# Both parts of x as one 512-column moving operand in the up projection of a decoder layer, with the residual's scale and offset in quarters

## The chip, the cores and the metric

The program runs on one core of a Trainium2 chip. The metric is the device time of one execution in microseconds (us), as a median of several runs. The engines in this text: PE does the matmuls (PEld its weight loads), DVE is the vector engine, ACT the scalar engine, POOL the GpSimd, and SP issues most of the DMAs. Each engine works through its own queue in order and waits on semaphores for the others.

## The reference, cut to what matters

One layer with sequence 256 and width 1024; everything is float32.

```python
x = layer_norm(ALPHA * x + mix, ln1_g, ln1_b)            # mix: attention, conv and pooling heads times w_out
up = causal_dwconv(x @ w_up, ffn_conv_w) + ffn_conv_b    # 1024 -> 2 * 2816, then width-3 taps along the sequence
u, g = split(up, 2)
ff = (u * silu(g)) @ w_down                              # 2816 -> 1024
x = layer_norm(ALPHA * x + ff, ln2_g, ln2_b)
```

## The kernel before

**Precision.** A product of float32 matrices is made from parts. `split(raw, hi, lo)` (lines 121 to 123) writes `hi`, a copy rounded to the fast matmul format, on ACT and `lo = raw - hi` on DVE. `mm3` (line 149) then issues three matmuls: hi by hi, hi by lo, lo by hi. So each weight tile of 128x1024 costs one ACT instruction (line 122) and one DVE instruction (line 123), and x itself is held as `xh` and `xl`.

**The up projection.** It has 22 column blocks j, each with two halves: s = 0 for u and s = 1 for g. `up_mm(j, s)` (line 460) runs over k = 0..7 with the weight part as the stationary 128x128 operand and 256 columns of `xh` or `xl` moving: 3 x 8 matmuls into one half of a PSUM bank, and u and g of one j share that bank. Block 0 is made apart (`up_first`), in plain float32, right after the first LayerNorm.

**The taps and the gate.** `taps(j, s)` (line 480) reads the bank: ACT writes `y` from it (line 485), DVE adds the two delayed taps, again from the bank (lines 486, 487). `gate_silu` (ACT, line 491) and `gate_out` follow: DVE makes `f` (line 495), ACT rounds it into `mh` (line 122), DVE makes `ml` (line 123).

**The down projection.** `down(k, t, p)` uses `mh[k]` and `ml[k]` as stationary operand and 512 columns of the down weights as moving operand. It trails the up projection by five blocks. For the last seven blocks only rows t = 0 are done at once. The matmuls of rows t = 1 for these blocks come in three pieces at the very end, and block 21 is the last in each.

**What sets the order.** The program is written as a list of blocks, each with its PE work, then work for the other engines that is written behind the PE work of the next block (`late`, lines 653 to 667): first the taps of the block before, then as many weight splits (`wsplit`) as a look-ahead of seven blocks asks for, then the gate. So on ACT and on DVE the taps, the weight splits and the gate of one j stand in a fixed order. From j = 6 to j = 20 three weight tiles are split for each j, from j = 1 to 5 and for j = 21 two.

**The first LayerNorm.** `ln1_rows` (DVE) normalises, `ln1_turn` (PE) transposes into PSUM, `ln1_cols` applies scale and offset by column into `xf` (line 444 on ACT for rows t = 0, line 446 on DVE for rows t = 1), `ln1_split` writes `xh` and `xl`. Beside that, `ln1_x` (lines 453, 454) applies scale and offset to the residual rows `xr` on POOL, one multiply and one add of 128x1024 for each t. `xr` is next read at the end, in the second LayerNorm's residual (line 360).

Of the kernel before, what the change touches and what calls it, by code (L numbers as in the profile page):

```python
# [17 lines left out]
P = 128  # L18
# [38 lines left out]
def trunk(ctx, tc, a_qk, a_v, a_cp, a_out, a_up, a_down, x, par, tab, lnp, out):  # L57
# [8 lines left out]
    def bank():  # L66
        return ps.tile([P, 512], F32, name="bank")
# [86 lines left out]
    tb = cp.tile([NB + 1, GW + NH], F32, name="tb")  # L154
    xh = cp.tile([P, KD, S], F32R, name="xh")
    xl = cp.tile([P, KD, S], F32R, name="xl")

# [263 lines left out]

    def ln1_rows(t):
        mv = norm_stats(t)
        for c in range(0, D, S):
            nc.vector.tensor_scalar(xr[:, t, c:c + S], xr[:, t, c:c + S], mv[:, 0:1], mv[:, 2:],
                                    op0=ALU.subtract, op1=ALU.mult)
# [9 lines left out]
    def ln1_cols(t, hf):  # L436

        ts = slice(t * P, (t + 1) * P)
        for i in range(4):
            k = 4 * hf + i  # L440
            src = t_ps[t, hf][:, i * P:(i + 1) * P]
            g, b = (prm[:, C_LN + r * KD + k:C_LN + r * KD + k + 1] for r in range(2))
            if t == 0:
                nc.scalar.activation(xf[:, k, ts], src, AF.Identity, scale=g, bias=b)
            else:
                nc.vector.tensor_scalar(xf[:, k, ts], src, g, b, op0=ALU.mult, op1=ALU.add)
# [4 lines left out]

    def ln1_x(t):
        nc.gpsimd.tensor_mul(xr[:, t], xr[:, t], gb[0][:, 0])  # L453
        nc.gpsimd.tensor_add(xr[:, t], xr[:, t], gb[0][:, 1])

# [3 lines left out]

    def up_mm(j, s):  # L460
        h, l = W.pop(("ug"[s], j))
        if s == 0:
            u_ps[j] = bank()
        for k in range(KD):
            ws = slice(k * P, (k + 1) * P)
            mm3(u_ps[j][:, s * S:(s + 1) * S], h[:, ws], l[:, ws], xh[:, k], xl[:, k], k == 0, k == KD - 1)

# [12 lines left out]
    def taps(j, s):  # L480
        c = s * NJ + j
        w = [prm[:, C_FW + 3 * c + i:C_FW + 3 * c + i + 1] for i in range(3)]
        src = u_ps[j][:, s * S:(s + 1) * S]
        y = ys[j, s] = tmp(f"y{s}")
        nc.scalar.activation(y, src, AF.Identity, scale=w[2], bias=prm[:, C_FB + c:C_FB + c + 1])  # L485
        nc.vector.scalar_tensor_tensor(y[:, 1:], src[:, :S - 1], w[1], y[:, 1:], op0=ALU.mult, op1=ALU.add)  # L486
        nc.vector.scalar_tensor_tensor(y[:, 2:], src[:, :S - 2], w[0], y[:, 2:], op0=ALU.mult, op1=ALU.add)  # L487
# [104 lines left out]
    for i in range(FIRST):  # L592
# [4 lines left out]
    block(L(w_out_last, 1, 0), (), [L(rs, 1, 0)])  # L597
    block(seq(L(ln1_turn, 0, 0), L(w_out_last, 1, 1)), (), [L(ln1_cols, 0, 0), L(rs, 1, 1)])
    block(seq(L(ln1_turn, 0, 1), L(w_out_last, 1, 2)), (),
          [L(ln1_cols, 0, 1), L(rs, 1, 2), L(ln1_rows, 1)], now=True, more=False)  # L600
    steps = list(enumerate((k, s) for s in range(2) for k in range(KD)))
    block(seq(L(up_first, 0, steps[:12]), L(ln1_turn, 1, 0)), (),
          [L(ln1_cols, 1, 0)], now=True, more=False)
    block(seq(L(up_first, 0, steps[12:]), L(ln1_turn, 1, 1)), (),
          [L(ln1_cols, 1, 1)] + [L(ln1_split, t, hf) for hf in range(2) for t in range(NT)],
          now=True, more=False)
# [134 lines left out]
```

## Time and profile before

| what | value |
| --- | --- |
| device time, 3 runs | median 294.5 us (293.94, 294.5, 296.25) |
| the profiled execution | 293.62 us, of which the span of the trace is 291.8 us |
| PE busy | 282.5 us, 97% of the span |
| PEld busy | 260.8 us, 89% |
| DVE busy | 222.7 us, 76% |
| ACT busy | 157.8 us, 54% |
| POOL busy | 41.1 us, 14% |
| TensorE clock granted | 0.996 of full speed |
| HBM read | 54.89 MB at a mean of 192 GB/s |

Matmuls overlap, so a matmul's own duration (282 ns for 256 columns) is longer than the step from one start to the next, and it is the step that counts. The busy share is over the whole span: what DVE and ACT do within the up projection has to be read from a stretch of it.

### The profile page before, as it was taken

The page shows a single profiled execution, that of the slowest core. Times are in us where ns is not written, and L with a number is a line of the kernel's source. Part 1 is how long each engine was busy: PE and PEld are TensorE (multiplying, and loading weights), DVE is VectorE, ACT ScalarE, POOL GpSimd, SP SyncE. Part 2 cuts the span into 40 slices and gives each one's busy share as a digit, 9 for nine tenths or more (in the row PEclk, how much of TensorE's full clock was granted, in tenths as well). Part 3 has the DMA queues.
Part 4 walks back from the last instruction along what each step waited for, and adds up shares of the span by engine and source line. Part 5 has one row for each costly group of instructions (what it writes and reads, how often), then busy time and mean ns, then how long its engine had stood idle before and what let it go on. Part 6 is the DMA issues. An engine that isn't in the chain of part 4 may idle for free.

```text
span 291.8 us, 5033 instructions
## 1 busy us (share of the span) xinstructions
PE 282.5 (97%) x2034; PEld 260.8 (89%) x2034; DVE 222.7 (76%) x384; ACT 157.8 (54%) x261; POOL 41.1 (14%) x43
## 2 busy tenths in 40 slices
PE   8999999999999999999999999999999999999990
PEld 7899779988888999999999999999999999999880
DVE  2876575797947699998988888888767867768575
ACT  3864746856512294266766666666555665665100
POOL 1020004860000279900000000000000000000011
PEclk9999999999999999999999999999999999999998
DMA  7999951234990169273737474847374552100011
GB/s 258 405 358 418 418 213 46 101 146 153 337 350 25 46 207 387 84 290 144 287 146 275 159 287 144 290 146 290 144 286 147 186 227 86 77 2 0 0 75 72
DMA packets 9367, 56.28 MB, mean 193 GB/s; under 512 B 1069, under 2 KB 1333, under 8 KB 3712
## 3 DMA queue, kind: packets, MB, share of 16 engines
q1 hardware_dynamic: 7920, 50.99, 46.5%
q0 software_dynamic: 1136, 4.58, 4.4%
q10 hardware_dynamic: 288, 0.39, 0.4%
q8 instruction: 16, 0.26, 0.3%
q14 instruction: 7, 0.06, 0.1%
HBM read 54.89 MB, written 1.06 MB: 192 GB/s over the span
## 4 chain that ended last, share of the span: by engine, by line
PE 79%; DVE 8%; ACT 4%; issue 4%; DMA 2%; POOL 1%; POOLq 0%; SPq 0%; DVEq 0%
PE bank L151 75%; DVE lo L123 3%; PE bank L474 2%; DMA raw<-a_qk 2%; DVE pr L242 2%; ACT pr L234 2%; ACT hi L122 2%; DVE lg L231 1%; PE bank L434 1%; PE bank L261 1%; DVE stat L366 1%; DVE xr L360 0%; DVE xr L521 0%; POOLq L737 0%; POOL mv L399 0%
## 5 line engine op out<-in xcount | busy, mean ns | idle before, releaser
L123 DVE TENSOR_TENSOR lo<-raw,hi 128x1024 fp32r<-128x1024 f32 (+2 forms) x95 | 113.8, 1210 | 23.6 <-ACT hi L122 23.3
L151 PE MATMUL bank<-xh,hi 128*128 128x256 f32 x462 | 130.3, 282 | 0.2 <-ACT hi L122 0.2
L151 PE MATMUL bank<-xh,lo 128*128 128x256 f32 x462 | 129.1, 279 | 0.2 <-DVE lo L123 0.2
L151 PE MATMUL bank<-xl,hi 128*128 128x256 f32 x462 | 129.0, 279 | 0.0
L122 ACT ACTIVATE hi<-raw 128x1024 fp32r<-128x1024 f32 (+2 forms) x95 | 95.4, 1018 | 4.5 <-DMA raw<-a_v 2.2
L151 PEld LDWEIGHTS bank<-xh,hi 128*128 128x128 f32 x462 | 87.1, 188 | 2.3 <-ACT hi L122 1.2
L151 PEld LDWEIGHTS bank<-xl,hi 128*128 128x128 f32 x462 | 87.1, 188 | 0.7
L151 PEld LDWEIGHTS bank<-xh,lo 128*128 128x128 f32 x462 | 87.0, 188 | 0.4 <-DVE lo L123 0.4
L151 PE MATMUL bank<-hi,mh 128*128 128x512 f32 (+1 forms) x133 | 49.3, 371 | 0.0
L151 PE MATMUL bank<-lo,mh 128*128 128x512 f32 (+1 forms) x133 | 49.2, 370 | 0.0
L151 PE MATMUL bank<-hi,ml 128*128 128x512 f32 (+1 forms) x133 | 49.0, 368 | 0.0
L485 ACT ACTIVATE y<-bank,prm 128x256 f32<-128x256 f32 x44 | 24.6, 559 | 25.8 <-PE bank L151 13.6
L399 POOL TENSOR_TENSOR mv<-mv,half 128x1 f32<-128x1 f32 x4 | 3.1, 774 | 186.3 <-DVE mv L398 186.3
L151 PEld LDWEIGHTS bank<-hi,ml 128*128 128x128 f32 x133 | 25.1, 188 | 4.3
L151 PEld LDWEIGHTS bank<-hi,mh 128*128 128x128 f32 x133 | 25.1, 189 | 3.7
L151 PEld LDWEIGHTS bank<-lo,mh 128*128 128x128 f32 x133 | 25.1, 188 | 3.5
L486 DVE SCALAR_TENSOR_TENSOR y<-bank,prm,y 128x255 f32<-128x255 f32 x44 | 21.0, 478 | 8.7 <-ACT y L485 8.6
L487 DVE SCALAR_TENSOR_TENSOR y<-bank,prm,y 128x254 f32<-128x254 f32 x44 | 21.2, 481 | 1.6
L122 ACT ACTIVATE mh<-f 128x256 fp32r<-128x256 f32 x22 | 9.2, 418 | 24.3 <-DVE f L495 24.3
L123 DVE TENSOR_TENSOR ml<-f,mh 128x256 fp32r<-128x256 f32 x22 | 11.0, 500 | 10.6 <-ACT mh L122 10.6
L491 ACT ACTIVATE sg<-y 128x256 f32<-128x256 f32 x22 | 9.2, 419 | 13.8 <-DVE y L487 13.8
L453 POOL TENSOR_TENSOR xr<-xr,lnp 128x1024 f32<-128x1024 f32 x2 | 13.4, 6702 | 3.1 <-DMA lnp<-lnp 3.1
(93 smaller groups left out, 201.9 us busy)
## 6 DMA issues: line engine op xcount, KB each, us to landing
raw<-a_up SPq DMA_DIRECT2D x22, 1024.0 KB, 4.8
raw<-a_down SPq DMA_DIRECT2D x11, 1024.0 KB, 5.6
raw<-a_qk SPq DMA_DIRECT2D x7, 640.0 KB, 7.2
raw<-a_cp SPq DMA_DIRECT2D x4, 1024.0 KB, 14.5
raw<-a_out SPq DMA_DIRECT2D x4, 1024.0 KB, 5.2
raw<-a_v SPq DMA_DIRECT2D x2, 1024.0 KB, 8.3
lnp<-lnp POOLq DMA_DIRECT2D x4, 512.0 KB, 4.6
bias<-g_dr POOLq DMA_DIRECT2D x1, 1024.0 KB, 13.6
```

Of the source, the lines that this page charges most:

```text
L122: nc.scalar.activation(hi, raw, AF.Copy)
L123: nc.vector.tensor_sub(lo, raw, hi.bitcast(F32))
L151: nc.tensor.matmul(o, l, r, start=start and i == 0, stop=stop and i == 2, skip_group_check=skip)
L234: nc.scalar.activation(pr[:, a:b], lg[:, a:b], AF.Exp, bias=st[:, t:t + 1], scale=-1.0, accum_out=st[:, 2 + t:3 + t])
L242: nc.vector.tensor_scalar(pr[:, a:b], pr[:, a:b], st[:, 4 + t:5 + t], None, op0=ALU.mult)
L399: nc.gpsimd.tensor_tensor(mv[:, 2:], mv[:, 2:], half, op=ALU.pow)
L453: nc.gpsimd.tensor_mul(xr[:, t], xr[:, t], gb[0][:, 0])
L474: nc.tensor.matmul(u_ps[0][:, c:c + P], part(("ug"[s], 0))[:, k * P:(k + 1) * P], xf[:, k, t * P:(t + 1) * P], start=t == 0 and n == 0, st ...
L485: nc.scalar.activation(y, src, AF.Identity, scale=w[2], bias=prm[:, C_FB + c:C_FB + c + 1])
L486: nc.vector.scalar_tensor_tensor(y[:, 1:], src[:, :S - 1], w[1], y[:, 1:], op0=ALU.mult, op1=ALU.add)
L487: nc.vector.scalar_tensor_tensor(y[:, 2:], src[:, :S - 2], w[0], y[:, 2:], op0=ALU.mult, op1=ALU.add)
L491: nc.scalar.activation(ys[j, 2], ys.pop((j, 1)), AF.Silu)
```

## The change

The two parts of x now stand side by side in one tile, `xp[P, k, part, S]`, and `xh` and `xl` are its two views. In `up_mm` the hi part of the weights is loaded once for each k and multiplied by 512 moving columns, hi and lo of x together, into a whole bank. The lo part of the weights is multiplied by 256 columns, the hi part of x, into the first half of that bank. The bank then holds two partial sums side by side. `taps` adds them: ACT copies the second half to `e`, DVE adds `e` to the first half in the bank, and then the three tap instructions follow as before. Each (j, s) has a bank of its own. The residual's scale and offset are written in quarters of 256 columns behind the blocks j = 8 to 15, and the parameters of the second LayerNorm are loaded behind block 16. In the first LayerNorm, `ln1_cols` for rows t = 1 alternates between DVE and ACT, and the two `ln1_split` of rows t = 0 stand earlier.

```diff
--- before.py
+++ after.py
@@ -37,6 +37,7 @@
 KEEP = 7
 FIRST = 2
 WARM = 23
+LATE = 8
 
 
 PIECES = (((0, 512), (512, 512)), ((0, 512), (512, 256), (768, 256)))
@@ -152,8 +153,9 @@
                              skip_group_check=skip)
 
     tb = cp.tile([NB + 1, GW + NH], F32, name="tb")
-    xh = cp.tile([P, KD, S], F32R, name="xh")
-    xl = cp.tile([P, KD, S], F32R, name="xl")
+
+    xp = cp.tile([P, KD, 2, S], F32R, name="xp")
+    xh, xl = xp[:, :, 0], xp[:, :, 1]
 
     zero = cp.tile([P, P], BF16, name="zero")
     nc.vector.memset(zero, 0.0)
@@ -419,8 +421,11 @@
 
     stats = [wk.tile([P, 4, 6], F32, name="stat") for _ in range(NT)]
 
-    def ln1_rows(t):
+    def ln1_rows(t, then=()):
         mv = norm_stats(t)
+
+        for f in then:
+            f()
         for c in range(0, D, S):
             nc.vector.tensor_scalar(xr[:, t, c:c + S], xr[:, t, c:c + S], mv[:, 0:1], mv[:, 2:],
                                     op0=ALU.subtract, op1=ALU.mult)
@@ -440,7 +445,7 @@
             k = 4 * hf + i
             src = t_ps[t, hf][:, i * P:(i + 1) * P]
             g, b = (prm[:, C_LN + r * KD + k:C_LN + r * KD + k + 1] for r in range(2))
-            if t == 0:
+            if t == 0 or i % 2:
                 nc.scalar.activation(xf[:, k, ts], src, AF.Identity, scale=g, bias=b)
             else:
                 nc.vector.tensor_scalar(xf[:, k, ts], src, g, b, op0=ALU.mult, op1=ALU.add)
@@ -449,21 +454,25 @@
         ks, ts = slice(4 * hf, 4 * hf + 4), slice(t * P, (t + 1) * P)
         split(xf[:, ks, ts], xh[:, ks, ts], xl[:, ks, ts])
 
-    def ln1_x(t):
-        nc.gpsimd.tensor_mul(xr[:, t], xr[:, t], gb[0][:, 0])
-        nc.gpsimd.tensor_add(xr[:, t], xr[:, t], gb[0][:, 1])
+    def ln1_x(t, q):
+        cs = slice(q * S, (q + 1) * S)
+        nc.gpsimd.tensor_mul(xr[:, t, cs], xr[:, t, cs], gb[0][:, 0, cs])
+        nc.gpsimd.tensor_add(xr[:, t, cs], xr[:, t, cs], gb[0][:, 1, cs])
 
 
     acc2 = [[], []]
     gt = {}
 
     def up_mm(j, s):
+
+
         h, l = W.pop(("ug"[s], j))
-        if s == 0:
-            u_ps[j] = bank()
+        o = u_ps[j, s] = bank()
         for k in range(KD):
             ws = slice(k * P, (k + 1) * P)
-            mm3(u_ps[j][:, s * S:(s + 1) * S], h[:, ws], l[:, ws], xh[:, k], xl[:, k], k == 0, k == KD - 1)
+            nc.tensor.matmul(o, h[:, ws], xp[:, k], start=k == 0, stop=False, skip_group_check=True)
+            nc.tensor.matmul(o[:, :S], l[:, ws], xp[:, k, 0], start=False, stop=k == KD - 1,
+                             skip_group_check=True)
 
     def up_first(t, steps):
 
@@ -480,7 +489,14 @@
     def taps(j, s):
         c = s * NJ + j
         w = [prm[:, C_FW + 3 * c + i:C_FW + 3 * c + i + 1] for i in range(3)]
-        src = u_ps[j][:, s * S:(s + 1) * S]
+        if j == 0:
+            src = u_ps[0][:, s * S:(s + 1) * S]
+        else:
+
+            o = u_ps.pop((j, s))
+            e, src = tmp("e"), o[:, :S]
+            nc.scalar.activation(e, o[:, S:], AF.Copy)
+            nc.vector.tensor_add(src, src, e)
         y = ys[j, s] = tmp(f"y{s}")
         nc.scalar.activation(y, src, AF.Identity, scale=w[2], bias=prm[:, C_FB + c:C_FB + c + 1])
         nc.vector.scalar_tensor_tensor(y[:, 1:], src[:, :S - 1], w[1], y[:, 1:], op0=ALU.mult, op1=ALU.add)
@@ -595,14 +611,14 @@
     block(L(w_out_last, 0, 0), last, [L(rs, 0, 0)], hold=4)
     block(L(w_out_last, 0, 1), (), [L(rs, 0, 1), L(ln1_rows, 0)])
     block(L(w_out_last, 1, 0), (), [L(rs, 1, 0)])
-    block(seq(L(ln1_turn, 0, 0), L(w_out_last, 1, 1)), (), [L(ln1_cols, 0, 0), L(rs, 1, 1)])
+    block(seq(L(ln1_turn, 0, 0), L(w_out_last, 1, 1)), (), [L(ln1_cols, 0, 0), L(rs, 1, 1), L(ln1_split, 0, 0)])
     block(seq(L(ln1_turn, 0, 1), L(w_out_last, 1, 2)), (),
-          [L(ln1_cols, 0, 1), L(rs, 1, 2), L(ln1_rows, 1)], now=True, more=False)
+          [L(ln1_cols, 0, 1), L(rs, 1, 2), L(ln1_rows, 1, [L(ln1_split, 0, 1)])], now=True, more=False)
     steps = list(enumerate((k, s) for s in range(2) for k in range(KD)))
     block(seq(L(up_first, 0, steps[:12]), L(ln1_turn, 1, 0)), (),
           [L(ln1_cols, 1, 0)], now=True, more=False)
     block(seq(L(up_first, 0, steps[12:]), L(ln1_turn, 1, 1)), (),
-          [L(ln1_cols, 1, 1)] + [L(ln1_split, t, hf) for hf in range(2) for t in range(NT)],
+          [L(ln1_cols, 1, 1), L(ln1_split, 1, 0), L(ln1_split, 1, 1)],
           now=True, more=False)
     steps = list(enumerate((k, s) for k in range(KD) for s in range(2)))
     block(L(up_first, 1, steps), (),
@@ -614,11 +630,14 @@
     for j in range(NJ):
         gate = [L(gate_silu, j), L(gate_out, j)]
         if j == 0:
-            block(seq(), (), [L(ln_rows, 0), L(taps, 0, 0), L(taps, 0, 1), L(ln1_x, 0), L(ln1_x, 1),
-                              L(ln_rows, 1)], gate)
+            block(seq(), (), [L(ln_rows, 0), L(taps, 0, 0), L(taps, 0, 1)], gate)
         else:
             block(L(up_mm, j, 0), [("u", j)], [L(taps, j, 0)])
-            block(L(up_mm, j, 1), [("g", j)], [L(taps, j, 1)], gate)
+
+            late_x = [L(ln1_x, *divmod(j - LATE, 4))] if 0 <= j - LATE < 8 else []
+            if j == LATE + 8:
+                late_x = [L(ln_rows, 1)]
+            block(L(up_mm, j, 1), [("g", j)], [L(taps, j, 1)] + late_x, gate)
         if j >= LAG:
             down_unit(j - LAG)
     for k in range(NJ - LAG, NJ):
```

**On DVE, in the up projection, around the taps of j = 8** (`lo` are weight splits, `y0` and `y1` the taps of u and g, `f` and `ml` the gate). Before:

```order
L495 TENSOR_TENSOR f_1855<-y0_1823,sg_1853 128x256
L123 TENSOR_TENSOR ml_117<-f_1855,mh_116 128x256
L123 TENSOR_TENSOR lo_1885<-raw_1647,hi_1884 128x1024
L486 SCALAR_TENSOR_TENSOR y0_1912<-bank_1859,prm_105,y0_1912 128x255
L487 SCALAR_TENSOR_TENSOR y0_1912<-bank_1859,prm_105,y0_1912 128x254
L123 TENSOR_TENSOR lo_1917<-raw_1647,hi_1916 128x1024
L486 SCALAR_TENSOR_TENSOR y1_1932<-bank_1859,prm_105,y1_1932 128x255
L487 SCALAR_TENSOR_TENSOR y1_1932<-bank_1859,prm_105,y1_1932 128x254
L123 TENSOR_TENSOR lo_1937<-raw_1574,hi_1936 128x1024
L495 TENSOR_TENSOR f_1946<-y0_1912,sg_1944 128x256
```

Now:

```order
L511 TENSOR_TENSOR f_1784<-y0_1749,sg_1782 128x256
L124 TENSOR_TENSOR ml_116<-f_1784,mh_115 128x256
L124 TENSOR_TENSOR lo_1806<-raw_1591,hi_1805 128x1024
L499 TENSOR_TENSOR bank_1788<-bank_1788,e_1826 128x256
L502 SCALAR_TENSOR_TENSOR y0_1829<-bank_1788,prm_104,y0_1829 128x255
L503 SCALAR_TENSOR_TENSOR y0_1829<-bank_1788,prm_104,y0_1829 128x254
L124 TENSOR_TENSOR lo_1834<-raw_1591,hi_1833 128x1024
L499 TENSOR_TENSOR bank_1809<-bank_1809,e_1849 128x256
L502 SCALAR_TENSOR_TENSOR y1_1852<-bank_1809,prm_104,y1_1852 128x255
L503 SCALAR_TENSOR_TENSOR y1_1852<-bank_1809,prm_104,y1_1852 128x254
L124 TENSOR_TENSOR lo_1859<-raw_1527,hi_1858 128x1024
L511 TENSOR_TENSOR f_1868<-y0_1829,sg_1866 128x256
```

One sum in the bank stands ahead of each pair of taps, and nothing stands between the sum and the taps that read ACT's `y`.

**On ACT, in the same place** (`hi` are weight splits). Before:

```order
L122 ACTIVATE mh_116<-f_1855 128x256
L122 ACTIVATE hi_1884<-raw_1647 128x1024
L485 ACTIVATE y0_1912<-bank_1859,prm_105 128x256
L122 ACTIVATE hi_1916<-raw_1647 128x1024
L485 ACTIVATE y1_1932<-bank_1859,prm_105 128x256
L122 ACTIVATE hi_1936<-raw_1574 128x1024
```

Now:

```order
L123 ACTIVATE mh_115<-f_1784 128x256
L123 ACTIVATE hi_1805<-raw_1591 128x1024
L498 ACTIVATE e_1826<-bank_1788 128x256
L501 ACTIVATE y0_1829<-bank_1788,prm_104 128x256
L123 ACTIVATE hi_1833<-raw_1591 128x1024
L498 ACTIVATE e_1849<-bank_1809 128x256
L501 ACTIVATE y1_1852<-bank_1809,prm_104 128x256
L123 ACTIVATE hi_1858<-raw_1527 128x1024
```

The copy `e` stands directly ahead of `y`, and `y` reads the bank that DVE's sum writes. The weight split that comes next stands behind `y`.

**On POOL, behind the first LayerNorm** (each row's waits in brackets). Before:

```order
L399 TENSOR_TENSOR mv_1175<-mv_1175,half_103 128x1 [waits DVE_49]
L355 DMA lnp_1295<-lnp 128x1024 x2
L453 TENSOR_TENSOR xr_1026<-xr_1026,lnp_1295 128x1024 [waits DMASW5_49,DMASW4_49,PE_49]
L454 TENSOR_TENSOR xr_1026<-xr_1026,lnp_1295 128x1024 [waits DMASW6_49,Pool_49]
L453 TENSOR_TENSOR xr_1026<-xr_1026,lnp_1295 128x1024 [waits DVE_49,PE_49]
L454 TENSOR_TENSOR xr_1026<-xr_1026,lnp_1295 128x1024 [waits Pool_49]
L355 DMA lnp_1310<-lnp 128x1024 [waits Pool_49]
```

Now:

```order
L401 TENSOR_TENSOR mv_1176<-mv_1176,half_102 128x1 [waits DVE_49]
L357 DMA lnp_1286<-lnp 128x1024 x2
L459 TENSOR_TENSOR xr_1025<-xr_1025,lnp_1286 128x256 [waits DMASW5_49,DMASW4_49,PE_49]
L460 TENSOR_TENSOR xr_1025<-xr_1025,lnp_1286 128x256 [waits DMASW6_49,Pool_49]
L459 TENSOR_TENSOR xr_1025<-xr_1025,lnp_1286 128x256 [waits PE_49]
L460 TENSOR_TENSOR xr_1025<-xr_1025,lnp_1286 128x256 [waits Pool_49]
```

The PE wait is on the transposes of the first LayerNorm. Six more such pairs follow directly. No row of them waits on a block of the up projection, and POOL has nothing else in its queue there.

## Rows read from the trace of the kernel before

**Rows 1.** The page: busy time, share of the span, instructions of each engine.
```profile
PE 282.5 (97%) x2034; PEld 260.8 (89%) x2034; DVE 222.7 (76%) x384; ACT 157.8 (54%) x261; POOL 41.1 (14%) x43
```
**Rows 2.** Chain of waits: start, length (us), what; the longest piece.
```profile
105.97 167.71 PE bank L151 x1227
```
**Rows 3.** Timeline, PE: start, duration (us), out<-in; 512 columns, then 256.
```profile
79.73 0.39 PE L151 MATMUL bank<-lo,mh 128*128 128x512 f32 x1
...
92.19 0.39 PE L151 MATMUL bank<-hi,ml 128*128 128x512 f32 x1
...
169.94 0.28 PE L151 MATMUL bank<-xh,hi 128*128 128x256 f32 x1
...
175.54 0.39 PE L151 MATMUL bank<-hi,mh 128*128 128x512 f32 x1
```
**Rows 4.** Timeline, DVE, j = 2 (two weight splits); idle and releaser in brackets.
```profile
126.79 0.42 DVE L495 TENSOR_TENSOR f<-y,sg 128x256 f32<-128x256 f32 x1
...
132.28 0.42 DVE L495 TENSOR_TENSOR f<-y,sg 128x256 f32<-128x256 f32 x1
```
**Rows 5.** Timeline, DVE, j = 6 (three weight splits).
```profile
148.76 0.42 DVE L495 TENSOR_TENSOR f<-y,sg 128x256 f32<-128x256 f32 x1
149.66 0.43 DVE L123 TENSOR_TENSOR ml<-f,mh 128x256 fp32r<-128x256 f32 x1 [0.48 <-ACT mh L122]
150.61 1.23 DVE L123 TENSOR_TENSOR lo<-raw,hi 128x1024 fp32r<-128x1024 f32 x1 [0.53 <-ACT hi L122]
151.75 0.48 DVE L486 SCALAR_TENSOR_TENSOR y<-bank,prm,y 128x255 f32<-128x255 f32 x1
152.27 0.48 DVE L487 SCALAR_TENSOR_TENSOR y<-bank,prm,y 128x254 f32<-128x254 f32 x1
...
155.84 0.42 DVE L495 TENSOR_TENSOR f<-y,sg 128x256 f32<-128x256 f32 x1
```
**Rows 6.** Timeline, ACT, the second half of j = 6.
```profile
152.78 0.56 ACT L485 ACTIVATE y<-bank,prm 128x256 f32<-128x256 f32 x1 [0.80 <-DVE y L487]
153.25 1.05 ACT L122 ACTIVATE hi<-raw 128x1024 fp32r<-128x1024 f32 x1
```
**Rows 7.** Groups by line: count, busy us, mean ns, idle before and releasers.
```profile
L485 ACT ACTIVATE y<-bank,prm 128x256 f32<-128x256 f32 x44 | 24.6, 559 | 25.8 <-PE bank L151 13.6 <-DVE y L487 10.7
...
L338 DVE TENSOR_TENSOR cz<-bank,cx 128x256 f32<-128x256 f32 x2 | 0.8, 416 | 0.0
...
L337 ACT ACTIVATE cx<-bank 128x256 f32<-128x256 f32 x2 | 0.7, 374 | 1.2 <-PE bank L151 1.2
```
**Rows 8.** Timeline, DVE, j = 0, beside POOL's work on the residual.
```profile
113.42 0.48 DVE L486 SCALAR_TENSOR_TENSOR y<-bank,prm,y 128x255 f32<-128x255 f32 x1 [0.64 <-ACT y L485]
...
114.37 3.33 DVE L123 TENSOR_TENSOR lo<-raw,hi 128x1024 fp32r<-128x1024 f32 x1
117.62 2.61 DVE L495 TENSOR_TENSOR f<-y,sg 128x256 f32<-128x256 f32 x1
120.72 2.07 DVE L123 TENSOR_TENSOR ml<-f,mh 128x256 fp32r<-128x256 f32 x1 [0.48 <-ACT mh L122]
```
**Rows 9.** Timeline, POOL and ACT in the same stretch.
```profile
104.11 10.03 POOL L453 TENSOR_TENSOR xr<-xr,lnp 128x1024 f32<-128x1024 f32 x1 [3.10 <-DMA lnp<-lnp]
114.22 2.40 POOL L454 TENSOR_TENSOR xr<-xr,lnp 128x1024 f32<-128x1024 f32 x1
...
115.80 0.42 ACT L491 ACTIVATE sg<-y 128x256 f32<-128x256 f32 x1
```
**Rows 10.** Timeline, the end: DVE's last f, PE's block 21, PE's last matmul.
```profile
270.51 0.43 DVE L495 TENSOR_TENSOR f<-y,sg 128x256 f32<-128x256 f32 x1 [0.54 <-ACT sg L491]
...
272.82 0.39 PE L151 MATMUL bank<-hi,mh 128*128 128x512 f32 x1
...
283.85 0.28 PE L151 MATMUL bank<-hi,ml 128*128 128x256 f32 x1
```
**Rows 11.** Windows at the end: busy by engine, then granted clock, DMA share, GB/s.
```profile
288.00:290.00 2.00, 0.00 (x0) 0.00 (x0) 0.57 (x2) 0.00 (x0) 0.00 (x0) 0.83 0.72 262
```

## The prediction, before the changed kernel had run

> **What bounds the kernel now.** I read the page first: PE is busy 97% of the span, DVE 76%, ACT 54% [rows 1]. Then the chain of waits: from 105.97 us on it is one piece of 167.71 us on PE, the whole up and down projection but the end [rows 2]. So a microsecond saved on PE counts at once, as long as DVE and ACT keep up. Whether they do is read from DVE's timeline in that stretch, and it is what decides here.
>
> The gate's `f` of each j is a good marker on DVE. With two weight splits a j takes 132.28 - 126.79 = 5.49 us [rows 4], with three 155.84 - 148.76 = 7.08 us [rows 5]. For PE the steps are (175.54 - 169.94) / 48 = 0.117 us for a 256-column matmul and (92.19 - 79.73) / 55 = 0.227 us for a 512-column one [rows 3]. So PE needs 48 x 0.117 = 5.60 us for an up projection of one j, and 12 x 0.227 = 2.72 us more where a down projection follows, 8.32 us. DVE has 0.1 us of slack per j in j = 1 to 5 and 1.24 us from j = 6 on. These 5.49 and 7.08 us aren't all work: DVE and ACT hand results to and fro, and DVE idles 0.48 us for `mh` and 0.53 us for `hi` in each j [rows 5]. It is a chain of two engines, and it ends at j = 21 with `f` at 270.51; PE starts block 21 of the down projection at 272.82 [rows 10]. The chain is 270.51 + 0.90 (from f to ml, [rows 5]) = 271.41, so it is only 1.4 us early there.
>
> **PE's part of the change.** For each of 336 pairs (21 j, two halves, eight k) three 256-column matmuls become one of 512 and one of 256: 3 x 0.117 = 0.350 us against 0.227 + 0.117 = 0.343 us. That is 336 x 0.0066 = 2.2 us less on PE. The columns streamed are the same, so the third weight load that goes was hidden beside matmuls. It is a gain only where PE is the bound.
>
> **The sum of the halves.** It adds 42 copies on ACT and 42 sums on DVE. The copy is priced by L337, also 256 columns from a bank: 0.374 us [rows 7]. It waits for PE alone and runs beside DVE's weight split ahead of it, so I cost it at nothing. The cover is DVE's `lo`, 1.23 us [rows 5]; without it the copy would cost its 0.374 us. The sum is nearest to L338, which takes a bank and an SBUF tile: 0.416 us [rows 7]; no row writes a bank from DVE. I take 0.42, between 0.37 (ACT's copy) and 0.56 (ACT's `y` of 256 columns, [rows 7]).
>
> The larger cost is the order. Before, ACT's `y` was ready when DVE came to the taps, since ACT had made it beside `ml` and `lo`. Now `y` reads what DVE's sum writes, and DVE's next instructions read `y`. DVE can do nothing in between, since its queue is in order. Such a wait stands in the trace once, at j = 0, where the second `y` had to follow DVE's taps on the same bank: DVE idle 0.64 us [rows 8]. In pieces: `y` lasts 0.56 us and starts 0.03 us after DVE's end at 152.75 [rows 5, 6]. So one (j, s) costs 0.42 + 0.03 + 0.56 + 0.03 = 1.04 us and one j 2.08 us on the DVE and ACT chain. The weight split behind doesn't hide it: ACT's `hi` stands behind `y`, starts 0.47 us after it and takes 1.05 [rows 6], so `lo` can start 1.96 us after the sum began, when the taps have just ended.
>
> So a j takes 5.49 + 2.08 = 7.57 us with two splits, 7.08 + 2.08 = 9.16 with three, and 9.16 - 1.14 + 0.54 = 8.56 for j = 21, which has one split less and the wait for `sg` [rows 5, 10]. PE would need 5.49 and 8.21. **The chain of DVE and ACT becomes the bound.** Bank waits don't add: from block 5 on, with four banks taken by the down projection, PE may be two j ahead of the taps at most, which makes PE wait and not the chain.
>
> **POOL and the first LayerNorm.** In before, POOL's work on the residual holds DVE up: `lo` takes 3.33 us instead of 1.23, `f` 2.61 instead of 0.42, `ml` 2.07 instead of 0.43 [rows 5, 8]. Writing it behind blocks 8 to 15 doesn't move it: no row of POOL's queue waits on these blocks, so it starts as before, near 104.11. The quarters help all the same: one holds DVE for some 2.40 / 4 = 0.6 us [rows 9]. While DVE ran without a gap, POOL's first multiply took 10.03 us [rows 9], so POOL comes in at the taps of j = 0. `f` of j = 0 can't start before ACT's `sg` has ended, at 116.25 [rows 9]. I add two quarters and take 117.5 for the start of the periods; the bounds are 116.25 and, with collisions as before, 117.62 + 2.19 + 1.64 = 121.4. The reordered splits and the alternating columns I cost at nothing: PE runs through there without a gap [rows 2], and DVE is behind for other reasons afterwards. If that cover went, it would show in the same bounds.
>
> **The sum.** Last `f`: 117.5 + 5 x 7.57 + 15 x 9.16 + 8.56 = 301.3 us. Block 21 on PE starts 0.90 us later, at 302.2. From there to the end of the span it was 291.8 - 272.82 = 19.0 us: 321.2. One more term: PE now idles 6 to 7 us ahead of block 21 (8.56 us for a j less the 1.36 us that block 20 takes, six steps of 0.227). After its last matmul at 283.85 the granted clock was still full until 288 and fell in the next 2 us, to a mean of 0.83 [rows 10, 11], so block 21 may begin at the lower level, 1.2 GHz. The 11.3 us of matmuls from 272.82 on would take up to 11.3 us more; no row shows how soon the clock comes back, and I take 2. Span 323.2, which is 31.4 us more than before. The profiled execution took 293.62 us, so this gives 325.0; it is 0.88 us under the median of the runs shown, which leads to **325.5 us** against 294.5.
>
> On the price of the sum in the bank, the Trainium skill (Perfetto Trace Analysis, Optimizing Scalar/DVE Operations) gives DVE about 125 ns of overhead per instruction on PSUM, and about twice that as profiled latency. With 256 columns at the 0.96 GHz that the Trainium skill gives for DVE (VectorE: DVE Perf Modes, Specifications) I estimate 0.52 us by it, where the row with a bank as input says 0.416; by it the total would be 42 x 0.10 = 4 us higher.
>
> **Rivals.**
> - *PE stays the bound* (other side). If ACT and DVE found other work in the new waits, only DVE's 0.84 us of sums per j would count, and from j = 6 on 1.24 us are free. Decisive point: the addition must stay under 8.21 - 7.08 = 1.1 us per j. Then PE's 2.2 us come through: 294.5 - 2.2 = 292.3. For it: DVE's 76%. Against it: both queues are in order, and the sum, `y` and taps stand directly behind each other. 5%.
> - *Half of it is hidden* (1.04 us per j): 117.5 + 5 x 6.53 + 15 x 8.21 + 7.5 = 280.8 for `f`, some 21 us less, 304. 8%.
> - *Separate banks free ACT.* ACT's `y` waited 10.7 us in all for DVE's taps on the shared bank [rows 7], 0.80 us per j [rows 6]. Each half now has a bank of its own. If this wait were on the chain, 15 x 0.80 = 12 us would come off: 313.5. Against it: DVE went on with `lo` meanwhile and didn't idle. 4%. The Trainium skill (PSUM — Partial Sum Buffer, PSUM bank collisions raise a hardware error) says that two engines may never be at one bank at once, so accesses must be ordered even without shared data; the row's wait agrees. By that rule the change frees u from g, and pays with four visits to one bank (copy, sum, y, taps) that can't overlap.
> - *The clock stays low after PE's new gaps*, so that the end costs its full 11.3 us: 335. 4%.
>
> **How the numbers follow.** The forecast has the other 79%. Its own range: the sum's price 42 x (-0.05 to +0.14) = -2 to +6, hand-overs 84 x 0.03 = 2.5 either way, POOL -1 to +4, the clock -2 to +9. Not all at once: 317 to 339. With the third rival and part of the second, 308 to 340 holds some 8 in 10. About 1%, 3 us, is what a measurement of this kernel tells from no change. Faster by more needs PE's gain and more: 2%. Within 1% is the first rival: 5%. Slower: 93%.
>
> **What would show it.** Right: DVE's two tap lines wait 0.6 us on ACT's `y` 42 times, some 26 us; a j lasts 7.6 and 9.2 us on DVE; the chain of waits runs through sum, `y`, taps and splits instead of one long PE piece; PE is busy some 280 us in a longer span, with gaps from block 5 on; POOL's quarters lie near 104 to 122 us. Wrong: taps that don't wait for `y`, or a sum in the bank that is much cheaper or dearer than 0.42 us.

## The result, and the profile after the change

The changed kernel takes **329.84 us** (median of 4 runs, 328.98 to 330.73), the kernel before 294.22 us on the same chip (4 runs, 293.36 to 296.25): a ratio of 1.121, 95% interval 1.1166 to 1.1254. The profiled execution took 329.2 us, of which the span of the trace is 327.4. Times and ratios leave out runs over 1.5% above the fastest of their kernel, which concerns one run of the reordered kernel below, the one whose trace is shown.

The page's first line answers to [rows 1]. PE has gone from 97% to 90% of its span, and neither DVE nor ACT has taken the first place: no engine is full.

```profile
PE 295.4 (90%) x1698; PEld 248.8 (76%) x1698; DVE 237.5 (73%) x422; ACT 172.1 (53%) x307; POOL 41.5 (13%) x55
```

The chain of waits tells more. Its shares of the span by line, the largest first, stand below. The long piece on PE [rows 2] is gone. Of the listed shares DVE holds some 41% (`lo`, the two taps, the sum `bank`, `f`) and ACT some 21% (`hi`, `y`, `mh`), in 627 short pieces that alternate.

```profile
by line: DVE lo L124 24.8%; PE bank L152 16.7%; ACT hi L123 10.3%; ACT y L501 7.5%; issue 6.5%; DVE y L502 4.6%; DVE y L503 4.6%; DVE bank L499 4.5%; ACT mh L123 2.8%; DVE f L511 2.4%; DVE pr L244 1.7%; ACT pr L236 1.7%; PE bank L164 0.8%; 
```

One j of the up projection with three weight splits, on DVE (start, duration, what; idle and releaser in brackets), answers to [rows 5]. From `f` to `f` it is 166.44 - 157.13 = 9.31 us, where it was 7.08. No line stands between a sum and its tap, and the tap starts 1.06 us behind the sum (161.19 - 160.13).

```profile
157.13 0.42 DVE L511 TENSOR_TENSOR f<-y,sg 128x256 f32<-128x256 f32 x1
158.04 0.42 DVE L124 TENSOR_TENSOR ml<-f,mh 128x256 fp32r<-128x256 f32 x1 [0.48 <-ACT mh L123]
158.99 1.23 DVE L124 TENSOR_TENSOR lo<-raw,hi 128x1024 fp32r<-128x1024 f32 x1 [0.53 <-ACT hi L123]
160.13 0.42 DVE L499 TENSOR_TENSOR bank<-bank,e 128x256 f32<-128x256 f32 x1
161.19 0.48 DVE L502 SCALAR_TENSOR_TENSOR y<-bank,prm,y 128x255 f32<-128x255 f32 x1 [0.63 <-ACT y L501]
161.71 0.48 DVE L503 SCALAR_TENSOR_TENSOR y<-bank,prm,y 128x254 f32<-128x254 f32 x1
162.14 1.23 DVE L124 TENSOR_TENSOR lo<-raw,hi 128x1024 fp32r<-128x1024 f32 x1
163.28 0.43 DVE L499 TENSOR_TENSOR bank<-bank,e 128x256 f32<-128x256 f32 x1
164.35 0.48 DVE L502 SCALAR_TENSOR_TENSOR y<-bank,prm,y 128x255 f32<-128x255 f32 x1 [0.64 <-ACT y L501]
164.87 0.48 DVE L503 SCALAR_TENSOR_TENSOR y<-bank,prm,y 128x254 f32<-128x254 f32 x1
165.29 1.23 DVE L124 TENSOR_TENSOR lo<-raw,hi 128x1024 fp32r<-128x1024 f32 x1
166.44 0.42 DVE L511 TENSOR_TENSOR f<-y,sg 128x256 f32<-128x256 f32 x1
```

Before, the second tap of a half was followed by `lo` after 0.40 us (152.27 in [rows 5], and this line of the kernel before); now it is 0.43 (161.71 to 162.14):

```profile
152.67 1.22 DVE L123 TENSOR_TENSOR lo<-raw,hi 128x1024 fp32r<-128x1024 f32 x1
```

The same stretch on ACT, first half of the j, answers to [rows 6]: the copy `e` is done early, and then ACT, which has nothing it may do, waits 1.37 us for the sum, because DVE is still at `lo`.

```profile
158.86 0.36 ACT L498 ACTIVATE e<-bank 128x256 f32<-128x256 f32 x1
160.59 0.57 ACT L501 ACTIVATE y<-bank,prm 128x256 f32<-128x256 f32 x1 [1.37 <-DVE bank L499]
161.06 1.05 ACT L123 ACTIVATE hi<-raw 128x1024 fp32r<-128x1024 f32 x1
```

The groups by line (count, busy us, mean ns, idle before and its releasers) answer to [rows 7]. Each engine waits for the other: `y` waits 53.4 us for the sum, the first tap 27.2 us for `y`.

```profile
L501 ACT ACTIVATE y<-bank,prm 128x256 f32<-128x256 f32 x44 | 24.8, 564 | 58.6 <-DVE bank L499 53.4 <-DVE y L503 5.2
L502 DVE SCALAR_TENSOR_TENSOR y<-bank,prm,y 128x255 f32<-128x255 f32 x44 | 21.2, 483 | 27.2 <-ACT y L501 27.2
...
L499 DVE TENSOR_TENSOR bank<-bank,e 128x256 f32<-128x256 f32 x42 | 17.8, 425 | 0.0
L498 ACT ACTIVATE e<-bank 128x256 f32<-128x256 f32 x42 | 15.4, 368 | 0.0
```

The start, beside POOL, answers to [rows 8, 9]. The next three fences are DVE, the matching line of DVE in the kernel before, and POOL. The five `lo` behind the first LayerNorm take 8.48 us, where they took 5.76; POOL's quarter operations stretch from 0.74 to 1.6 or 1.7 us where they lie beside them.

```profile
106.45 8.48 DVE L124 TENSOR_TENSOR lo<-raw,hi 128x1024 fp32r<-128x1024 f32 x5 [0.17 <-ACT hi L123]
...
119.30 0.52 DVE L511 TENSOR_TENSOR f<-y,sg 128x256 f32<-128x256 f32 x1 [0.37 <-ACT sg L507]
```
```profile
106.12 5.76 DVE L123 TENSOR_TENSOR lo<-raw,hi 128x1024 fp32r<-128x1024 f32 x5
```
```profile
106.38 0.74 POOL L460 TENSOR_TENSOR xr<-xr,lnp 128x256 f32<-128x256 f32 x1 [1.33 <-DMA lnp<-lnp]
107.07 1.73 POOL L459 TENSOR_TENSOR xr<-xr,lnp 128x256 f32<-128x256 f32 x1
108.88 1.60 POOL L460 TENSOR_TENSOR xr<-xr,lnp 128x256 f32<-128x256 f32 x1
```

At the end DVE's last `f` starts at 305.25 us, and PE's block 21 follows at 306.18, which answers to [rows 10]. The timeline of PE shows 5.13 us of idle time ahead of it, and then steps of 0.43 us, where 512 columns had taken 0.23.

```profile
306.18 0.80 PE L152 MATMUL bank<-hi,mh 128*128 128x512 f32 x1 [5.13 <-ACT mh L123]
306.77 0.63 PE L152 MATMUL bank<-lo,mh 128*128 128x512 f32 x1
307.20 0.63 PE L152 MATMUL bank<-hi,ml 128*128 128x512 f32 x1
```

### The profile page after: what moved, and what is told of

Its sections match the earlier page's. It is cut to its first block, busy times and chain, and to the rows that moved or that the text cites. A ratio compares the mean times of both kernels' runs of the same rounds, so it can differ in the third digit from the quotient of the medians.

```text
span 327.4 us, 4500 instructions
## 1 busy us (share of the span) xinstructions
PE 295.4 (90%) x1698; PEld 248.8 (76%) x1698; DVE 237.5 (73%) x422; ACT 172.1 (53%) x307; POOL 41.5 (13%) x55
## 3 DMA queue, kind: packets, MB, share of 16 engines
HBM read 54.89 MB, written 1.06 MB: 171 GB/s over the span
## 4 chain that ended last, share of the span: by engine, by line
DVE 47%; ACT 24%; PE 20%; issue 6%; POOL 1%; POOLq 0%; DVEq 0%; ACTq 0%
DVE lo L124 25%; PE bank L152 17%; ACT hi L123 10%; ACT y L501 7%; DVE y L502 5%; DVE y L503 5%; DVE bank L499 5%; ACT mh L123 3%; DVE f L511 2%; DVE pr L244 2%; ACT pr L236 2%; PE bank L164 1%; DVE ml L124 1%; DVE lg L233 1%; PE bank L197 1%
## 5 line engine op out<-in xcount | busy, mean ns | idle before, releaser
L124 DVE TENSOR_TENSOR lo<-raw,hi 128x1024 fp32r<-128x1024 f32 (+2 forms) x95 | 115.1, 1223 | 23.3 <-ACT hi L123 23.2
L473 PE MATMUL bank<-xp,hi 128*128 128x512 f32 x336 | 122.0, 402 | 10.0 <-DVE y L503 8.4
L474 PE MATMUL bank<-xp,lo 128*128 128x256 f32 x336 | 95.6, 285 | 0.2 <-DVE lo L124 0.2
L473 PEld LDWEIGHTS bank<-xp,hi 128*128 128x128 f32 x336 | 64.1, 191 | 31.5 <-ACT hi L123 18.7
L474 PEld LDWEIGHTS bank<-xp,lo 128*128 128x128 f32 x336 | 64.6, 192 | 0.6 <-DVE lo L124 0.5
L152 PE MATMUL bank<-hi,mh 128*128 128x512 f32 (+1 forms) x133 | 51.2, 385 | 10.2 <-ACT mh L123 5.1
L501 ACT ACTIVATE y<-bank,prm 128x256 f32<-128x256 f32 x44 | 24.8, 564 | 58.6 <-DVE bank L499 53.4
L152 PE MATMUL bank<-lo,mh 128*128 128x512 f32 (+1 forms) x133 | 50.6, 380 | 2.4 <-DVE lo L124 2.3
L152 PE MATMUL bank<-hi,ml 128*128 128x512 f32 (+1 forms) x133 | 50.0, 376 | 0.0
L152 PE MATMUL bank<-xp,hi 128*128 128x256 f32 x252 | 46.4, 287 | 0.0
L502 DVE SCALAR_TENSOR_TENSOR y<-bank,prm,y 128x255 f32<-128x255 f32 x44 | 21.2, 483 | 27.2 <-ACT y L501 27.2
L152 PEld LDWEIGHTS bank<-xp,hi 128*128 128x128 f32 x252 | 39.3, 191 | 1.4 <-ACT hi L123 0.6
L152 PE MATMUL bank<-xp,lo 128*128 128x256 f32 x126 | 35.4, 281 | 0.0
L152 PEld LDWEIGHTS bank<-xp,lo 128*128 128x128 f32 x126 | 24.0, 190 | 0.0
L503 DVE SCALAR_TENSOR_TENSOR y<-bank,prm,y 128x254 f32<-128x254 f32 x44 | 21.2, 481 | 1.6
L499 DVE TENSOR_TENSOR bank<-bank,e 128x256 f32<-128x256 f32 x42 | 17.8, 425 | 0.0
```

What stands on the lines that cost most here:

```text
L124: nc.vector.tensor_sub(lo, raw, hi.bitcast(F32))
L152: nc.tensor.matmul(o, l, r, start=start and i == 0, stop=stop and i == 2, skip_group_check=skip)
L473: nc.tensor.matmul(o, h[:, ws], xp[:, k], start=k == 0, stop=False, skip_group_check=True)
L474: nc.tensor.matmul(o[:, :S], l[:, ws], xp[:, k, 0], start=False, stop=k == KD - 1, skip_group_check=True)
L499: nc.vector.tensor_add(src, src, e)
```

## The experiments

**Is it the order, or the amount of work?** My theory was the serial hand-over: the sum on DVE, `y` on ACT and the taps on DVE follow each other on two queues that run in order, so neither engine can use the time. The rivals were the mere amount of added work on DVE and ACT, and a shortage of banks, since each half of a j now takes a whole one. Each ratio is to the kernel before, run again beside the experiment (medians of 293.8 to 294.4 us). The first kernel leaves the copy and the sum out:

```
-            e, src = tmp("e"), o[:, :S]
-            nc.scalar.activation(e, o[:, S:], AF.Copy)
-            nc.vector.tensor_add(src, src, e)
+            src = o[:, :S]
```


> The changed kernel without the copy and the sum: the taps read the first 256 columns of the bank, so the lo part of x is left out of the result (its matmuls stay). Serial hand-over (sum, then y, then taps, each waiting for the one before) and plain added work on DVE and ACT both say that the chain of DVE and ACT falls back to 5.49 and 7.08 us per j and PE bounds again, with its 2.2 us of gain and the new start of the periods: 290 to 294 us. Shortage of banks (one for every j and half, held for two more operations) says that it stays above 320 us.

Measured: 297.0 us, ratio to before 1.0096 (1.0057 to 1.0134). A j lasts 5.49 and 7.08 us on DVE again, then PE's 8.30. So copy and sum make the loss; but it is 3 us more than I expected, and the kernel stays above the one before.

The second keeps the work and takes the hand-over away:

```
-            nc.vector.tensor_add(src, src, e)
+            scr = tmp("scr")
+            nc.vector.tensor_add(scr, e, e)
```


> The changed kernel with the copy kept and a sum of the same size on DVE, but of two SBUF tiles into a scratch tile that nobody reads: the same work, no hand-over from the sum to y (the lo part of x is left out of the result). Serial hand-over says: DVE has 0.84 us more per j, 6.33 us with two weight splits and 7.92 with three, so PE bounds again from j = 6 on and only j = 1 to 5 cost some 0.8 us each: 292 to 298 us, with the tap lines of DVE hardly waiting for ACT. Plain added work says: near the changed kernel, 320 to 332 us.

Measured: 300.4 us, ratio 1.0232 (1.0174 to 1.0291). That is 2.4 us above the range of the serial hand-over and far from that of plain work; PE waits 4.1 us for banks in this kernel, which comes up again below. DVE's timeline of one j:

```profile
158.26 0.42 DVE L512 TENSOR_TENSOR f<-y,sg 128x256 f32<-128x256 f32 x1
...
161.25 0.42 DVE L500 TENSOR_TENSOR scr<-e 128x256 f32<-128x256 f32 x1
161.59 0.48 DVE L503 SCALAR_TENSOR_TENSOR y<-bank,prm,y 128x255 f32<-128x255 f32 x1
162.10 0.48 DVE L504 SCALAR_TENSOR_TENSOR y<-bank,prm,y 128x254 f32<-128x254 f32 x1
162.50 1.22 DVE L124 TENSOR_TENSOR lo<-raw,hi 128x1024 fp32r<-128x1024 f32 x1
...
166.01 0.42 DVE L512 TENSOR_TENSOR f<-y,sg 128x256 f32<-128x256 f32 x1
```

The tap follows the sum after 0.34 us instead of 1.06, and waits for nothing. A j lasts 7.75 us; with two splits it is 6.10. The changed kernel's 9.29 us (its mean over j = 6 to 20) thus divide into 7.08 as before, 0.67 for the work and 1.54 for the order; its 7.54 with two splits into 5.49, 0.61 and 1.44. So seven tenths of the cost per j go with the order. This sum reads SBUF and not a bank, but it lasts the same 0.42 us.

The third keeps every operation and computes everything, in another order:

```
+            block(L(up_mm, j, 0), [("u", j)], [L(tsum, j, 0)],
+                  [L(gate_silu, j - 1), L(gate_f, j - 1), L(taps, j, 0), L(gate_split, j - 1)])
...
+            block(L(up_mm, j, 1), [("g", j)], [L(tsum, j, 1)] + late_x, [L(taps, j, 1)] + end)
```

(`tsum` is copy and sum, `taps` is `y` and the two taps; the first list stands ahead of a weight split, the second behind it; `end` is the gate of the last j.)

> Same operations as the changed kernel, all results computed, in another order on ACT and DVE: copy and sum of the halves ahead of a weight split, y and the two taps behind it, the gate of j one half later, so that y, sg and mh are made while DVE is at a lo. Serial hand-over says: a j costs DVE its work alone, two lo, four taps, two sums, f and ml, about 2 x 1.15 + 4 x 0.50 + 2 x 0.42 + 0.86 = 6.0 us with two splits and 7.15 with three; PE bounds from j = 6 on: 292 to 299 us, and the waits of the two tap lines for y fall from 53 us for both to under 10. Plain added work, or a shortage of banks, says 320 us or more.

Measured: 297.53 us, ratio 1.0116 (1.005 to 1.0182). The first tap waits 1.3 us in all for `y`, where it was 27.2. (The 53 us of the expectation are `y`'s wait for the sum.) One j of it on DVE:

```profile
153.88 0.42 DVE L518 TENSOR_TENSOR f<-y,sg 128x256 f32<-128x256 f32 x1
154.21 0.48 DVE L507 SCALAR_TENSOR_TENSOR y<-bank,prm,y 128x255 f32<-128x255 f32 x1
154.73 0.48 DVE L508 SCALAR_TENSOR_TENSOR y<-bank,prm,y 128x254 f32<-128x254 f32 x1
155.13 0.41 DVE L124 TENSOR_TENSOR ml<-f,mh 128x256 fp32r<-128x256 f32 x1
155.46 0.42 DVE L498 TENSOR_TENSOR bank<-bank,e 128x256 f32<-128x256 f32 x1
156.00 1.23 DVE L124 TENSOR_TENSOR lo<-raw,hi 128x1024 fp32r<-128x1024 f32 x1
157.15 0.48 DVE L507 SCALAR_TENSOR_TENSOR y<-bank,prm,y 128x255 f32<-128x255 f32 x1
...
160.66 0.42 DVE L518 TENSOR_TENSOR f<-y,sg 128x256 f32<-128x256 f32 x1
```

With the two sums in it a j lasts 160.66 - 153.88 = 6.78 us, less than the 7.08 of the kernel before: almost no bracket is left, because `y`, `sg` and `mh` are made while DVE has something else to do. The kernel with the sum in SBUF, below, has the same 6.78 us. The same work that made the kernel 36 us slower costs under 4 us in this order, so it isn't the amount. This order also takes away the waits for `mh` and `hi` that the kernel before has (0.48 and 0.53 us per j, [rows 5]), so it doesn't price the sums by themselves; the kernels with the sum aside and with the bare hand-over do that.

The fourth is the kernel before with the banks of the change and nothing else:

```
-        if s == 0:
-            u_ps[j] = bank()
+        o = u_ps[j, s] = bank()
```


> The kernel before, with a bank of its own for each half of a j (256 columns used), and nothing else changed. Shortage of banks as the cause says that this alone costs most of the difference, over 315 us. Serial hand-over and plain added work say no change, 293 to 296 us; y's 10.7 us of waits for the taps on the shared bank go, but PE bounds.

Measured: 299.14 us, ratio 1.017 (1.0124 to 1.0217). Order and work had said no change, banks over 315 us; it is neither. Banks don't explain the 36 us, but alone they cost 5, which I had missed. Two stretches of 5 us of its windows (busy us of PE, PEld, DVE, ACT, POOL, then the granted clock) show how: PE does 1.67 us of work in one, and the clock falls in the next.

```profile
135.00:140.00 5.00, 1.67 (x7) 0.83 (x7) 4.42 (x9) 3.15 (x7) 0.00 (x0) 1.00 0.34 85
140.00:145.00 5.00, 5.00 (x32) 5.00 (x31) 4.42 (x9) 3.15 (x6) 0.00 (x0) 0.66 0.88 334
```

The views of waits name the releaser (engine and line, waited for; us, times, longest). DVE is late there because of its delay beside POOL (once POOL is made late, below, the wait is gone), the down projection has just taken four banks, and PE stands until DVE's taps give one back:

```profile
PE bank L151 <- DVE y L486: 3.3, 2, 2.5
```

The wait of 3.3 us and a mean clock of 0.66 in 5 us, some 1.7 us of lost work, add up to the 5 us. The changed kernel without copy and sum waits the same way, for 2.2 us, and then has the same clock of 0.66; by the same estimate that is 3.9 us, enough for its unexpected 3 us.

**The hand-over by itself, and the other parts.** One kernel puts a hand-over into the kernel before, with next to no work:

```
+        if j:
+            nc.vector.tensor_scalar(src[:, :2], src[:, :2], 1.0, None, op0=ALU.mult)
         y = ys[j, s] = tmp(f"y{s}")
```


> The kernel before, and nothing of the change but the hand-over: ahead of ACT's y, DVE multiplies two columns of the bank by 1.0, so that y must wait for DVE, which stands at its lo and ml until then. Serial hand-over says: the tiny operation (I estimate 0.1 us) and y's 0.56 us come onto the chain of DVE and ACT twice per j. The runs give 7.54 - 6.10 = 1.44 us per j for the order alone, so a j takes 5.49 + 1.44 + 0.2 = 7.1 us with two splits and 8.7 with three, more than PE's 8.35: 308 to 316 us. Plain added work says 0.2 us more on DVE per j, which PE hides: 293 to 296 us.

Measured: **321.72 us**, ratio 1.0936 (1.0905 to 1.0967). A multiplication of two columns makes the kernel 27 us slower. Its rows on DVE:

```profile
163.67 0.16 DVE L485 TENSOR_SCALAR bank<-bank 128x2 f32<-128x2 f32 x1
164.46 0.48 DVE L488 SCALAR_TENSOR_TENSOR y<-bank,prm,y 128x255 f32<-128x255 f32 x1 [0.64 <-ACT y L487]
```

A j lasts 7.02 and 8.77 us, near the 7.1 and 8.7 expected. The total is above my range because I summed it too low: its last `f` starts at 297.52, and from there to the end of the span it is the same 22 us as in the changed kernel (327.4 - 305.25).

The other two parts of the change alone, on the kernel before (`ln1_x` in quarters behind blocks 8 to 15, `ln1_cols` and `ln1_split` as changed):

> The kernel before with the two other parts of the change alone: the residual in quarters written behind blocks 8 to 15, and the reordered splits and alternating columns of the first LayerNorm. That they are worth nothing says 293 to 296 us, with f of j = 0 between 117 and 120 us. That they explain part of the loss says over 297 us.

Measured: 294.76 us, ratio 1.0023 (0.999 to 1.0056). No change, as expected.

**Can a version beat the kernel before?** The reordered kernel still waits for banks (PE, 3.3 us). Writing the sum to SBUF gives a bank back after the sum:

```
-            e, src = tmp("e"), o[:, :S]
+            e, src = tmp("e"), tmp("x")
             nc.scalar.activation(e, o[:, S:], AF.Copy)
-            nc.vector.tensor_add(src, src, e)
+            nc.vector.tensor_add(src, o[:, :S], e)
```
This kernel also has 16 temporary tiles of 256 columns where the others have 12.

> The reordered kernel with the sum of the halves written to an SBUF tile, which y and the taps read: a bank is free after the sum and not after the taps, some 2.6 us earlier. If what is left over the kernel before (298.4 against 293.8 us) is PE's wait for banks near 138 to 146 us and the lower granted clock behind it, both shrink or go: 293 to 296 us. If it comes from elsewhere, it stays at 297 to 300.

> The reordered kernel with the sum in SBUF once more, in more rounds, beside the next one: 295 to 297 us, since PE still waits 1.6 us for a bank.

Measured: 296.0 and 295.69 us; over the second, larger set of runs the ratio is 1.0063 (1.004 to 1.0086). PE waits 1.6 us for banks instead of 3.3. Whether the time is below that of the reordered kernel the intervals don't tell. Then POOL's quarters made late in earnest:

```
+        nc.gpsimd.tensor_copy(junk, lastf[0][:, :2])
         nc.gpsimd.tensor_mul(xr[:, t, cs], xr[:, t, cs], gb[0][:, 0, cs])
```


> The same, and POOL's quarters made late in earnest: ahead of each quarter POOL copies two columns of the latest f, so that it waits for that j. DVE's first lo and f are then not held up, f of j = 0 comes some 4 to 6 us earlier than in the reordered kernel (124.2), PE finds its banks free, and from j = 8 on DVE has 8.30 - 6.78 = 1.5 us per j for the collisions: 291 to 294 us. If DVE's delay at the start costs nothing, the same time as the kernel with the sum in SBUF; if POOL's late work holds DVE up more than it has to spare, more than that.

> The same with POOL late, once more: PE waited for no bank in it, but its matmul steps were 0.234 us per 512 columns, 3 per cent longer than in the others, and already at 70 to 100 us, where the kernels do not differ. If that belonged to the run, this kernel is 1.5 to 3 us faster than the one without late POOL, 293 to 295 us. If it belongs to the kernel, 297 us again.

Measured: 297.52 and 297.01 us, the latter 1.0117 (1.0087 to 1.0147). PE waits for no bank any more, as meant, and yet the time is 1.3 us longer: all of PE's 512-column steps are 0.234 us in this kernel and 0.227 or 0.228 in the one above, in both of the runs of each. So it belongs to the kernel and not to the run. No version here beats the kernel before.

**The two small terms.** On the changed kernel, twenty useless matmuls ahead of block 21:

```
+        if k == NJ - 1:
+            block(L(dummies, 20))
         down_unit(k)
```


> The changed kernel with twenty 512-column matmuls of no use on PE (20 x 0.227 = 4.5 us) ahead of block 21 of the down projection, where PE idled 5.13 us; they read xp and write a bank that nobody reads. If the 2.0 us that block 21's first ten matmuls cost (0.43 us a step and not 0.23) came from the granted clock after the idle time, the steps are 0.23 from the start and the end comes 2 us earlier: 327 to 328.5 us. If something else slows these ten (their weights, their data), the steps stay at 0.43 and the time at 329 to 331.

Measured: 327.15 us, ratio to before 1.1129 (1.1102 to 1.1157), 2.7 us under the changed kernel; the spans of the two traces, 325.3 and 327.4, are 2.1 apart. PE's timeline:

```profile
301.58 4.72 PE L646 MATMUL bank<-xp 128*128 128x512 f32 x20
```
```profile
306.20 0.50 PE L152 MATMUL bank<-hi,mh 128*128 128x512 f32 x1
306.54 0.40 PE L152 MATMUL bank<-lo,mh 128*128 128x512 f32 x1
306.78 0.39 PE L152 MATMUL bank<-hi,ml 128*128 128x512 f32 x1
```

Block 21 starts 0.02 us later than in the changed kernel and its steps are 0.23 us from the second on. PE's last matmul starts at 317.38 instead of 319.47. The term was the clock.

And the late quarters on the changed kernel, the same two columns copied ahead of each:

> The changed kernel with POOL's quarters made late in earnest: ahead of each, POOL copies two columns of the latest f, so that it waits for that j. If POOL's quarters cost the start of the periods what the prediction added for them, f of j = 0 comes 1 to 3 us earlier than 119.3. Behind it the chain of DVE and ACT has nothing to spare, and there are 16 operations of POOL: if each holds a lo of DVE up by the 0.5 us seen beside j = 0, 330 to 336 us; if they fit into DVE's waits for y, 327 to 329.

Measured: 329.45 us, ratio 1.1235 (1.1192 to 1.1278), the changed kernel's time. DVE's start:

```profile
107.96 5.76 DVE L124 TENSOR_TENSOR lo<-raw,hi 128x1024 fp32r<-128x1024 f32 x5 [0.17 <-ACT hi L123]
...
118.10 0.42 DVE L515 TENSOR_TENSOR f<-y,sg 128x256 f32<-128x256 f32 x1 [0.65 <-ACT sg L511]
```

This run came to the five `lo` 1.5 us later than the changed kernel's; 0.55 us of that are slower matmul steps ahead of the LayerNorm (the last section shows them). From the start of the five `lo` to `f` it is 10.14 us, where it was 119.30 - 106.45 = 12.85: POOL costs the start 2.7 us, all of it in the five `lo` (8.48 against 5.76). Moved to j = 8 to 15, where the chain has nothing to spare, the quarters cost eight j 9.54 us instead of 9.29, 2.0 us in all. So it is neither of the two outcomes I had written down: the gain and the cost cancel.

## Why the prediction was right, step by step

Predicted were 325.5 us (308 to 340); 329.84 came. The last `f` was forecast at 301.3 and came at 305.25. The chain of DVE and ACT became the bound, by the hand-over that the prediction named. (Its last addition is off by 0.4: 325.0 + 0.88 is 325.9.)

- **The sum of the halves and its order**, 2.08 us per j: right in size and cause. Per j it is 7.54 - 5.49 = 2.05 with two splits and 9.29 - 7.08 = 2.21 with three. The inner division was different: of the 2.08 I took 0.84 for two sums and 1.24 for the hand-overs; the kernel with the sum aside shows some 0.64 and 1.5. An operation on DVE costs its queue less than its duration, since the next one starts 0.34 us after a sum of 0.425; and the wait costs more than the tap's bracket of 0.63.
- **The sum's price**: 0.42 taken, 0.425 measured. The estimate of 0.52 us from the Trainium skill (Perfetto Trace Analysis, Optimizing Scalar/DVE Operations) was too high here. The copy is 0.368 where the row said 0.374, and stays hidden beside `lo`, as costed.
- **Periods**: 7.57 forecast, 7.54 measured; 9.16 forecast, 9.29 measured; 8.56 forecast, 8.74 measured. The error of 0.13 in 15 j is 2.0 us of the whole error. The rows show where it lies: the two steps from sum to tap are 1.06 and 1.07 us where I took 1.04, the two from the second tap to the next `lo` 0.43 and 0.42 where the kernel before has 0.40, and `lo` to what follows is 0.01 to 0.02 us longer three times.
- **The start of the periods**: 117.5 forecast, 119.30 measured, 1.8 us. This term was mis-sized: I added 1.25 us for two quarters, and POOL costs 2.7. The price of a quarter was right, 0.6 us taken and (8.48 - 5.76) / 5 = 0.54 measured; the number was not, since all five `lo` were held up. I had expected POOL to find DVE without a gap there, as in [rows 9]; in quarters it takes turns with them. The other 0.3 us: without POOL's 2.7 this `f` would have come at 116.6 and not at 116.25. The reordered splits and columns, costed at nothing, moved nothing where PE bounds: 294.76 us for these two parts alone. In the changed kernel they weren't tried apart.
- **The end**: `f` to block 21 is 0.93 us (0.90 forecast), from there to the end of the span 21.2 (19.0 + 2). PE idled 5.13 us ahead of block 21, where I had 6 to 7. The clock's 2 us were a guess between 0 and 11.3, and a lucky one; the run with useless matmuls confirms the term, with a last matmul 2.1 us earlier.
- **PE's gain** of 2.2 us can't be seen, since PE no longer bounds. Where PE bounds, the period goes from 8.35 us (rows of the kernel before near 230 us) to 8.30: some 1 us in 21 j, half of what I took. One sign of mine missed: PE was to be busy some 280 us, and the page says 295.4. PE's own periods didn't grow, as the kernels that hide the sum show; I can't split the 15 us.
- **Bank waits don't add**: right for the changed kernel, where PE stands and the chain does not. PE waits 12.5 us for DVE's taps there, and from 140 to 150 us its granted clock is 0.50, while DVE's periods stay at 7.54 and 9.3 us. But the rival "PE stays the bound" at 292.3 left them out: with these banks PE stands 1.6 to 4.1 us near 136 us in every version that hides the sum but the one with late POOL, and mostly runs at a lower clock behind it. So even with the sum hidden, the kernels that compute everything came to 295.7 to 297.5, and never under the kernel before.
- **Separate banks free ACT**: fell. `y` now waits 53.4 us for the sum instead of 10.7 for the taps. "Half of it is hidden" fell too, since the 2.08 us come through whole; the clock came back, so its rival fell as well.

The sum of the errors: 1.8 for the start, 2.0 for 15 periods, 0.2 for j = 21, 0.2 for the end, 4.2 us together, the span's 327.4 against 323.2.

## What to carry to other kernels

When a change makes an operation of engine A read what engine B has just written, and B's next instruction read A's result, look at what stands in both queues between the two: if nothing does, and the chain of the two engines bounds or comes to bound, each such exchange costs the whole length of both operations, however small the first is (0.79 us with a first operation of 0.16, from 163.67 to 164.46 above). Put the producer ahead of a long independent instruction and the consumer behind it; here that was worth 32 us with the same instructions. Count the buffers too: PE's waits for banks cost nothing in the changed kernel and showed when PE came to bound again.

## What the runs showed of the hardware that I had not expected

- **Who got through when DVE and POOL both worked in SBUF went with the size of POOL's pieces.** As one multiplication of 1024 columns, POOL's first operation took 10.03 us, while DVE's five `lo` behind each other took 5.76 in the kernel before; in pieces of 256 columns POOL's took 1.6 to 1.7 us each and DVE's five `lo` 8.48. The kernels with the banks alone and with the hand-over alone, whose POOL work is whole, have 5.76 too; the one with the other two parts alone, in quarters, has 8.24. Those with quarters also have the new order of the LayerNorm, but with it and without POOL beside them the five take 5.76 again (107.96 above).
- **Two kernels with one more tile of two columns had matmul steps about 3% longer.** The two kernels with the tile `junk` (8 bytes per partition, allocated once) have, in all three of their profiled runs, 512-column steps of 0.234 us, also at 73 to 94 us, where their work is that of the others, the granted clock is 1.00 and POOL has made no copy into the tile yet. All eleven profiled runs without the tile have 0.227 there. The same 102 matmuls in the chain of waits (start, length), first of the reordered kernel with the sum in SBUF, then of that one with late POOL; the changed kernel has 20.71 too, and 21.26 with `junk`:

```profile
72.15 20.71 PE bank L152 x102
```
```profile
72.92 21.26 PE bank L152 x102
```

  The cause is open. That the tile shifts the addresses of those behind it is my guess; the tile was not tried without the rest of that edit.
- **The clock after an idle stretch.** After 5.13 us without a matmul PE's steps were those of the lower level, 1.2 GHz, with a mean granted clock of 0.53 in 306 to 311 us, and back at 0.23 us from 310.6 on, after 4.4 us of work. A wait of 2.2 us near 136 us (the kernel without the sum) and two of 3.3 together, the longer 2.5 (the kernel with the banks alone), were followed by a mean of 0.66 in 140 to 145; after one of 1.6 us (the sum in SBUF) it stayed at 1.00. A stretch filled with useless matmuls left the clock at 1.00.
